# A hybrid encoder step on one core: factors of the scan queued behind splits of weights, the last 32 products with tokens stationary, eight warming products

## The chip, the cores and the metric

The kernel runs on one core of a Trainium2 chip. The metric is the device time of one execution in microseconds (us), as the median of several runs. TensorE (PE) multiplies, VectorE (DVE) and ScalarE (ACT) work element by element, GpSimd (POOL) does small copies and sums, and SyncE (SP) issues most of the DMAs. Each engine runs its own queue in the order that the scheduler gave it, and waits there for semaphores.

## The reference

One layer for 256 prompt tokens and 32 sample tokens, 288 columns in all, with 2048 features:

```python
xn   = rmsnorm(x, norm_mix_pre)
proj = xn @ w_in             # columns: u_pool 1024 | z 2048 | xBC 2560 | dt 32
y_pool = pool_mixer(u, ...)  # trailing means, one matmul per group
y_ssd  = ssd_mixer(z, xbc, dt_raw, ...)   # conv, chunked scan, gate silu(z), norm
x    = x + rmsnorm(concat[y_pool, y_ssd] @ w_out, norm_mix_post)
up   = causal_dwconv(rmsnorm(x, norm_ffn_pre) @ w_up)
x    = x + rmsnorm((silu(gate) * val) @ w_down, norm_ffn_post)
# inside the scan, per head, l and s positions of a chunk:
lmat  = exp(acum[l] - acum[s]) masked causally
y     = (C B^T * lmat) (x * dt) + C h_prev exp(acum) + D x
```

The outputs are y for both groups of tokens and the new states. Everything is in float32.

## The kernel before

Activations lie with features on the partitions and the 288 tokens along the free axis. A product in full precision is made of three: weights and activations are each split into a high part (`whi`, `xn`'s first half) and the rest (`wlo`), and `mm3` (L144 to L146) multiplies high by high, high by low and low by high. `split_w` makes the parts of a tile of weights in pieces of 1024 columns: ACT copies to the high part (L137), DVE subtracts for the rest (L138).

`project` computes 256 output features from all 2048 inputs: two fetched tiles of weights, four splits, 24 products of 288 columns per split, into two PSUM tiles `acc`. Projects 1 to 7 of the loop make the inner x of the scan; their results are evacuated by DVE (L359, L360, into `ebuf`), go through a convolution of four taps (`conv`, L372), a tanh and `xs` (L377, L378). Projects 8 to 15 make the gates z (evacuated at L555). Behind each project `scan(i)` runs, i being the project's number. The scan works on heads in fours, eight of them, with numbers q from 0 to 7:

- `four_in(q)` loads `gb` (log decays), `h0t` (state) and `xw` by SP, and makes the factors: `ce` (ACT Exp, DVE L489), `xw` (DVE L492, times dt), `m` (ACT Relu in twelve pieces and one Exp of 1664 columns at L499, DVE L501 times C B^T). It is called at the projects in SCAN_IN = {5, 6, 7, 8, 9, 11, 12, 13}.
- `four_out` issues 16 products `py` (L523) and adds them to xs on DVE (L528). At the projects in SCAN_OUT = {7, 9, 12, 14} two fours are put out, directly behind the project's last product on PE.

The scheduler orders the instructions of each engine by a simulation of its own; `tc.issue_after(x)` keeps what stands under it behind x in the order, `tc.high_priority(offset=...)` pulls it ahead, `tc.keep_in_program_order` fixes it. `last_in[0]` is the latest evacuation.

At the start, six calls of a product of ones (`idle`, L260, two passes of PE each) run until the first input is there. At the end, the last 256 output features of the down projection are computed apart: for the first six tiles of input all three products go to `low`; for the 16 others, low by high goes to `low` for all tokens, high by both parts of the activations goes to `run_a` for tokens 128 to 287 (L1172), and the same for tokens 0 to 127 to `run_b` (32 products of 256 columns, L1185, weights stationary). DVE adds these to `part` (L1115), ACT squares (L1118), a product with a column of constants (`mean`) sums over the features (`psum_f`, L1086), ACT takes the root (`rf`, L1100), DVE inverts. The tokens are turned to rows by PE (`pft`, L1080), and DVE scales and adds the residual (`y_out`, L1129), but one tile of 512 columns goes over PE: residual by identity (L1208) plus rows by diag(rf) (L1215). The part of the prompt tokens in each output tile b is 128 tokens in a row, b·128 to b·128 + 127.

## Time and profile before

| | before |
|---|---|
| median of 3 runs | 1233.65 us (1233.14 to 1234.08) |
| profiled execution, own time | 1235.27 us |
| its span | 1233.0 us |
| PE busy | 1225.3 us (99%) |
| DVE busy | 888.2 us (72%) |
| ACT busy | 670.2 us (54%) |
| POOL busy | 276.3 us (22%) |

The span is the time between the first and the last instruction of the profiled execution; its own time holds what lies around it too. In a row of the timeline the first number is the start in us from the beginning of the span, the second the duration from the first start to the last end, then the engine, the line, the operation and the tiles (out<-in); "x8" says that eight instructions in a row stand together, and brackets tell how long the engine stood idle before and what released it. A PE row's duration is longer than the distance to the next, since matmuls are pipelined.

### The profile page before, as it was taken

The page shows a single profiled execution, that of the slowest core. Times are in us where ns is not written, and L with a number is a line of the kernel's source. Part 1 is how long each engine was busy: PE and PEld are TensorE (multiplying, and loading weights), DVE is VectorE, ACT ScalarE, POOL GpSimd, SP SyncE. Part 2 cuts the span into 40 slices and gives each one's busy share as a digit, 9 for nine tenths or more (in the row PEclk, how much of TensorE's full clock was granted, in tenths as well). Part 3 has the DMA queues.
Part 4 walks back from the last instruction along what each step waited for, and adds up shares of the span by engine and source line. Part 5 has one row for each costly group of instructions (what it writes and reads, how often), then busy time and mean ns, then how long its engine had stood idle before and what let it go on. Part 6 is the DMA issues. An engine that isn't in the chain of part 4 may idle for free.

```text
span 1233.0 us, 25222 instructions
## 1 busy us (share of the span) xinstructions
PE 1225.3 (99%) x10059; PEld 1213.7 (98%) x10059; DVE 888.2 (72%) x1484; ACT 670.2 (54%) x1011; POOL 276.3 (22%) x427
## 2 busy tenths in 40 slices
PE   9999999999999999999999999999999999999998
PEld 9999999999999999999999999999999999999997
DVE  8899998989664599887776744446777777765555
ACT  8557787546554466645554544334555454554443
POOL 6395442131341200221211200001112121101110
PEclk9999999999999999999999999999999999999999
DMA  9668785466576555676655455555555555576763
GB/s 356 197 208 307 263 279 172 149 243 221 199 242 216 191 177 201 200 228 181 208 185 171 166 185 179 169 191 188 189 172 175 188 184 172 175 252 198 217 190 118
DMA packets 87589, 249.82 MB, mean 203 GB/s; under 512 B 45712, under 2 KB 51920, under 8 KB 65200
## 3 DMA queue, kind: packets, MB, share of 16 engines
q1 hardware_dynamic: 83184, 240.78, 58.3%
q0 software_dynamic: 3712, 6.95, 1.9%
q8 instruction: 78, 1.28, 0.4%
q10 hardware_dynamic: 576, 0.49, 0.1%
q14 instruction: 39, 0.32, 0.1%
HBM read 236.23 MB, written 11.95 MB: 201 GB/s over the span
## 4 chain that ended last, share of the span: by engine, by line
PE 63%; DMA 1%; DVE 1%; ACT 0%; issue 0%; DVEq 0%
PE acc L144 20%; PE acc L145 20%; PE acc L146 20%; DMA st<-xs_d 1%; PE acc_x L145 0%; PE acc_x L144 0%; PE acc_x L146 0%; PE run_a L1172 0%; PE low L1170 0%; PE run_b L1185 0%; DVE rm L247 0%; PE low L146 0%; PE low L145 0%; PE low L144 0%; DVE sh L836 0%; PE y_ps L1215 0%
## 5 line engine op out<-in xcount | busy, mean ns | idle before, releaser
L138 DVE TENSOR_TENSOR wlo<-raw,whi 128x1024 fp32r<-128x1024 f32 (+1 forms) x386 | 461.3, 1198 | 245.6 <-ACT whi L137 245.3
L137 ACT ACTIVATE whi<-raw 128x1024 fp32r<-128x1024 f32 (+1 forms) x386 | 396.9, 1031 | 349.2 <-PE acc L145 283.4
L145 PE MATMUL acc<-hn,whi 128*128 128x288 f32 x1360 | 382.9, 286 | 0.0
L146 PE MATMUL acc<-hn,wlo 128*128 128x288 f32 x1360 | 382.7, 286 | 0.0
L144 PE MATMUL acc<-hn,whi 128*128 128x288 f32 x1360 | 382.2, 286 | 0.3 <-ACT hn L926 0.3
L144 PEld LDWEIGHTS acc<-hn,whi 128*128 128x128 f32 x1360 | 254.2, 189 | 0.8 <-ACT hn L926 0.7
L145 PEld LDWEIGHTS acc<-hn,whi 128*128 128x128 f32 x1360 | 254.7, 189 | 0.1
L146 PEld LDWEIGHTS acc<-hn,wlo 128*128 128x128 f32 x1360 | 254.6, 189 | 0.0
L144 PE MATMUL acc<-xn,whi 128*128 128x288 f32 x686 | 197.2, 289 | 0.0
L145 PE MATMUL acc<-xn,whi 128*128 128x288 f32 x686 | 195.6, 287 | 0.0
L146 PE MATMUL acc<-xn,wlo 128*128 128x288 f32 x686 | 192.3, 287 | 0.6 <-DVE wlo L138 0.6
L144 PE MATMUL acc<-fa,whi 128*128 128x288 f32 x660 | 188.8, 286 | 0.0
L145 PE MATMUL acc<-fa,whi 128*128 128x288 f32 x660 | 188.8, 286 | 0.0
L146 PE MATMUL acc<-fa,wlo 128*128 128x288 f32 x660 | 188.8, 286 | 0.0
L980 POOL COPY fc_stage<-ebuf 128x4 f32<-128x4 f32 x88 | 28.7, 326 | 463.4 <-DVE ebuf L979 401.2
L144 PEld LDWEIGHTS acc<-xn,whi 128*128 128x128 f32 x686 | 130.1, 190 | 1.4 <-issue 0.9
L145 PEld LDWEIGHTS acc<-xn,whi 128*128 128x128 f32 x686 | 130.1, 190 | 0.3
L146 PEld LDWEIGHTS acc<-xn,wlo 128*128 128x128 f32 x686 | 128.3, 190 | 1.0 <-DVE wlo L138 1.0
L144 PEld LDWEIGHTS acc<-fa,whi 128*128 128x128 f32 x660 | 124.7, 189 | 0.0
L145 PEld LDWEIGHTS acc<-fa,whi 128*128 128x128 f32 x660 | 124.7, 189 | 0.0
L146 PEld LDWEIGHTS acc<-fa,wlo 128*128 128x128 f32 x660 | 124.7, 189 | 0.0
L984 ACT ACTIVATE fc<-ebuf,pf 128x290 f32<-128x290 f32 x88 | 54.4, 622 | 78.7 <-DVE ebuf L979 78.7
(312 smaller groups left out, 1799.8 us busy)
## 6 DMA issues: line engine op xcount, KB each, us to landing
raw<-in_w_up SPq DMA_DIRECT2D x80, 1024.0 KB, 4.8
raw<-in_w_in SPq DMA_DIRECT2D x38, 1024.0 KB, 5.1
raw<-in_w_down SPq DMA_DIRECT2D x32, 1024.0 KB, 4.8
raw<-in_w_out SPq DMA_DIRECT2D x23, 1024.0 KB, 5.1
raw<-in_w_down SPq DMA_DIRECT2D x16, 768.0 KB, 4.5
raw<-in_w_up SPq DMA_DIRECT2D x8, 896.0 KB, 4.7
gb<-g_d SPq DMA_DIRECT2D x8, 832.0 KB, 6.6
raw<-in_w_first SPq DMA_DIRECT2D x5, 768.0 KB, 8.5
```

Source lines behind the costliest of these rows:

```text
L137: act.activation(hi, raw[:, k : k + n, :], AF.Copy)
L138: dve.tensor_tensor(lo, raw[:, k : k + n, :], hi.bitcast(F32), op=ALU.subtract)
L144: pe.matmul(out, wh, hi, start=start, stop=False)
L145: pe.matmul(out, wh, lo, start=False, stop=False)
L146: pe.matmul(out, wl, hi, start=False, stop=stop)
L980: pool.tensor_copy(fc_stage[:, :, :, i], e[:, 256:324].rearrange("p (s c) -> p s c", c=34)[:, :, 0:2])
L984: act.activation(c, e[:, 0:290], AF.Identity, bias=pf[:, 3, i : i + 1], scale=pf[:, 0, i : i + 1])
```

## The change

Three parts.

1. `four_in` is split. It keeps the loads; a new `four_mul` makes the factors and takes a split of weights (`splits` collects ACT's copies) behind which they are issued, besides the latest evacuation. The first four of a pair is made at the second SCAN_IN project of the pair, behind the last split issued; the second at the SCAN_OUT project, behind the fourth last. In project 6 both are made, behind the last two splits.
2. In the last 32 products the tokens are stationary and the weights move, so that `run_b` holds tokens on the partitions. Its tokens are the even ones of the prompt, `run_a`'s the odd ones and the sample's. What `low` gave to the even tokens is copied by ACT (`even`) and added by two products with the identity. The square sum of these features comes from ACT's accumulator (`total`), that of the earlier ones from a product (`rb`); the gains of the last 256 features are loaded as a row (`g_row`, by POOL), and DVE multiplies by them (`fg`). The tile that goes over PE is made in two halves, and its output DMA is issued by ACT. Output tiles hold every second token.
3. The warming calls are eight instead of six.

```diff
+    splits = []
...
-                act.activation(hi, raw[:, k : k + n, :], AF.Copy)
+                splits.append(act.activation(hi, raw[:, k : k + n, :], AF.Copy))
...
-    for i in range(6):
+    for i in range(8):
         tc.keep_in_program_order(pe.matmul(idle, ones, ones, start=True, stop=True))
...
-        with tc.issue_after(last_in[0].ins):
+        return gb, xw, h0t, ce, m
+
+    def four_mul(q, gb, xw, h0t, ce, m, after):
+
+        with tc.issue_after(last_in[0].ins), tc.issue_after(after.ins):
             act.activation(ce, gb[:, :, 384:], AF.Exp)
...
-    ready = []
+    loads, ready = [], []
...
+    def four_next(after):
+        q, tiles = loads.pop(0)
+        ready.append((q, four_mul(q, *tiles, after)))
...
         if i in SCAN_OUT:
+            if loads:
+                four_next(splits[-4])
...
-            ready.append((q, four_in(q)))
+            loads.append((q, four_in(q)))
+            if len(loads) == 2:
+                four_next(splits[-2 if i == 6 else -1])
+                if i == 6:
+                    four_next(splits[-1])
...
+    g_row = ebuf[0][:, : 2 * P]
+    pool.dma_start(out=g_row, in_=g_last.broadcast_to([P, 2 * P]))
...
-                sp.dma_start(out=ft[2 * q + b][:, :n], in_=fd[b * P : (b + 1) * P, c])
+                sp.dma_start(out=ft[2 * q + b][:, :n], in_=fd[b:NP_:2, c])
...
     def run_of(a, c):
-        return a.rearrange("p s (r j) -> p s j r", r=2)[:, :, c.start // 2 : c.stop // 2, :]
+        return a[:, :, c].rearrange("p s c -> p c s")
...
+    even = [out_tile("even") for _ in range(2)]
+    for j in range(2):
+        act.activation(even[j][:, :P], part[KD - 2 + j][:, 0:NP_:2], AF.Copy)
...
-    for j in range(2):
-        c = slice(j * P, (j + 1) * P)
-        for i, (k, hi, lo) in enumerate(held):
+    for i, (k, hi, lo) in enumerate(held):
+        for s in range(2):
             tc.keep_in_program_order(
-                pe.matmul(pb[j], hi[:, c], run_of(f2[k], B), start=k == K_RUN, stop=k == HALF - 1)
+                pe.matmul(
+                    pb, f2[k][:, s, B], turns(hi),
+                    start=i + s == 0, stop=i == len(held) - 1 and s == 1,
+                )
             )
+        if i == 1:
+            for j in range(2):
+                tc.keep_in_program_order(
+                    pe.matmul(by_turns(pb)[:, j, :], even[j][:, :P], ident, start=False, stop=False)
+                )
...
+            act.activation(rb, p_f[1][:, 0:1], AF.Identity, bias=eps_t)
...
+    tc.keep_in_program_order(
+        dve.tensor_tensor(last[0][:, : 2 * P].rearrange("p (r j) -> p r j", r=2), by_turns(pb), halves(g_row), op=ALU.mult)
+    )
+    act.activation(sq[:, : 2 * P], pb, AF.Square, accum_out=total)
+    act.activation(rf[:, 0:1], total, AF.Sqrt, bias=rb, scale=1.0 / D_MODEL)
+    dve.reciprocal(rf[:, 0:1], rf[:, 0:1])
+    y_ps = [acc_ps.tile([P, 2 * P], F32, tag="acc", name="y_ps") for _ in range(2)]
...
+    for i, p_ in enumerate(y_ps):
+        pe.matmul(p_, diag, halves(ft[2])[:, i, :], start=False, stop=True)
+        act.activation(halves(xr[2])[:, i, :], p_, AF.Copy)
...
-    sp.dma_start(out=y_rows[:, 1, :], in_=xr[2])
+    act.dma_start(out=y_rows[:, 1, :], in_=xr[2])
```

**Where instructions stand, first place: project 9's end.** On DVE before, a four's factors (ce, xw, m) stand behind the first z of project 8 (acc_2063); these are the factors of the second four that project 9 puts out.

```order
L555 TENSOR_TENSOR z_2182<-acc_2063,rstd_124 128x288 [waits PE_49]
L489 TENSOR_TENSOR ce_2225<-ce_2225,bc_772 128x128
L492 TENSOR_TENSOR xw_2222<-xw_2222,tok_734 128x768 [waits DMAHW6_49,DMAHW4_49]
L501 TENSOR_TENSOR m_2226<-m_2226,cbt_795 128x1664 [waits Activation_49]
```

On DVE after, they stand behind both z of project 9 (acc_2241, acc_2242).

```order
L140 TENSOR_TENSOR wlo_2507<-raw_2504,whi_2506 128x1024 [waits DMAHW6_49,PE_49,Activation_49]
L561 TENSOR_TENSOR z_2359<-acc_2241,rstd_124 128x288 [waits PE_49]
L374 SCALAR_TENSOR_TENSOR conv_2170<-ebuf0_110,pah_122,conv_2170 128x291 [waits DVE_49]
L182 STREAM_TRANSPOSE blocks_1991<-xs_1980 128x288 [waits DMASW2_49,DMASW1_49,DMASW3_49,DMASW0_49,DVE_49]
L374 SCALAR_TENSOR_TENSOR conv_2187<-ebuf1_112,pah_122,conv_2187 128x291 [waits Activation_49,Pool_49]
L561 TENSOR_TENSOR z_2361<-acc_2242,rstd_124 128x288 [waits PE_49]
L495 TENSOR_TENSOR ce_2209<-ce_2209,bc_774 128x128
L498 TENSOR_TENSOR xw_2206<-xw_2206,tok_736 128x768 [waits DMAHW5_49,DMAHW3_49]
L507 TENSOR_TENSOR m_2210<-m_2210,cbt_797 128x1664
L140 TENSOR_TENSOR wlo_2511<-raw_2504,whi_2510 128x1024 [waits Activation_49]
```

On PE before, at the same place, from the project's last product to the second four's first:

```order
L146 MATMUL acc_2258<-xn_609,wlo_2324 128x288
L523 MATMUL py_2379<-m_2043,xw_2039 64x256 [waits DMAHW0_49,PE_49]
...
L523 MATMUL py_2380<-ce_2042,h0t_2037 64x32 x2
L523 MATMUL py_2381<-m_2226,xw_2222 64x256 [waits DMAHW4_49,PE_49]
L523 MATMUL py_2381<-m_2226,xw_2222 64x256
```

and after:

```order
L148 MATMUL acc_2242<-xn_611,wlo_2308 128x288
L529 MATMUL py_2381<-m_2045,xw_2041 64x256 [waits DMAHW0_49,PE_49]
...
L529 MATMUL py_2382<-ce_2044,h0t_2039 64x32 x2
L529 MATMUL py_2383<-m_2210,xw_2206 64x256 [waits DMAHW3_49,DVE_49,PE_49]
L529 MATMUL py_2383<-m_2210,xw_2206 64x256
```

The order on PE is the same, and the second four's first product has a wait for DVE that it had not. The same wait stands at the second four's first product in projects 12 and 14, where DVE has one split and the project's two z right ahead of the factors; in project 7 there is none.

**Second place: DVE at the evacuation of project 6** (ebuf4, ebuf5), before:

```order
L359 TENSOR_TENSOR ebuf4_673<-acc_1652,rstd_124 128x256 [waits PE_49]
L138 TENSOR_TENSOR wlo_1900<-raw_1897,whi_1899 128x1024 [waits DMAHW6_49,Activation_49]
L360 TENSOR_TENSOR ebuf4_673<-acc_1652,rstd_124 128x32
...
L359 TENSOR_TENSOR ebuf5_674<-acc_1653,rstd_124 128x256 [waits PE_49]
L360 TENSOR_TENSOR ebuf5_674<-acc_1653,rstd_124 128x32
L489 TENSOR_TENSOR ce_1817<-ce_1817,bc_772 128x128
L492 TENSOR_TENSOR xw_1814<-xw_1814,tok_734 128x768 [waits DMAHW7_49,DMAHW0_49]
L501 TENSOR_TENSOR m_1818<-m_1818,cbt_795 128x1664 [waits DMAHW3_49]
L138 TENSOR_TENSOR wlo_1904<-raw_1897,whi_1903 128x1024 [waits Activation_49]
```

and after:

```order
L361 TENSOR_TENSOR ebuf5_676<-acc_1637,rstd_124 128x256 [waits PE_49]
L362 TENSOR_TENSOR ebuf5_676<-acc_1637,rstd_124 128x32
L140 TENSOR_TENSOR wlo_1848<-raw_1841,whi_1847 128x1024 [waits Activation_49]
L495 TENSOR_TENSOR ce_1634<-ce_1634,bc_774 128x128
L498 TENSOR_TENSOR xw_1631<-xw_1631,tok_736 128x768 [waits DMAHW1_49,DMAHW0_49]
L507 TENSOR_TENSOR m_1635<-m_1635,cbt_797 128x1664
L495 TENSOR_TENSOR ce_1801<-ce_1801,bc_774 128x128
L498 TENSOR_TENSOR xw_1798<-xw_1798,tok_736 128x768 [waits DMAHW7_49,DMAHW0_49]
L140 TENSOR_TENSOR wlo_1902<-raw_1899,whi_1901 128x1024 [waits DMAHW6_49,Activation_49]
L379 SCALAR_TENSOR_TENSOR xs_1593<-tanh_1600,conv_1595 128x256 [waits Activation_49]
L380 SCALAR_TENSOR_TENSOR xs_1593<-tanh_1600,conv_1595 128x32
L507 TENSOR_TENSOR m_1802<-m_1802,cbt_797 128x1664 [waits DMAHW3_49,Activation_49]
```

Before, two splits of project 7 are done around one four's factors. After, one split comes ahead of both fours' factors, and the next two are between and behind them.

**Third place: PE's last rows**, before:

```order
L1185 MATMUL run_b<-fa,whi 128x256 x13
L1086 MATMUL psum_f<-mean,fsq 128x1
L1208 MATMUL y_ps<-xr,ident 128x512
L1080 MATMUL pft<-ident,part 128x128
L1086 MATMUL psum_f<-mean,fsq 128x1
L1080 MATMUL pft<-ident,part 128x128
L1215 MATMUL y_ps<-ft,diag 128x512
```

and after:

```order
L1221 MATMUL psum_f<-mean,fsum 128x1
L1203 MATMUL run_b<-whi,fa 128x256 x16
L1240 MATMUL y_ps<-xr,ident 128x256 x2
L1243 MATMUL y_ps<-ft,diag 128x256 x2
```

Sums and transposes of run_b's tokens are no longer there, and the two products of y are four of half the width.

More of the change, by code (lines that the diff above doesn't have):

```diff
@@ L60, in body @@
     w_down,
+    g_last,
     y_rows,
@@ L1046, in body @@
             t = apool.tile([P, 512], F32, tag="a", name="xr")
-            sp.dma_start(out=t, in_=x1d[b * P : (b + 1) * P, 512 * q : 512 * (q + 1)])
+            sp.dma_start(out=t, in_=x1d[b:NP_:2, 512 * q : 512 * (q + 1)])
             xr.append(t)
@@ L1057, in body @@
     A, B = slice(P, NT), slice(0, P)
-    AB = (((1, P, P), (2, NP_, NS)), ((0, 0, P),))
+    AB = ((1, slice(1, NP_, 2)), (2, slice(NP_, NT)))
     rf = const.tile([P, 3], F32, name="rf")
+    g_row = ebuf[0][:, : 2 * P]
+    out_tile = lambda name: fp.tile([P, 290], F32, tag="fc", bufs=6, name=name)
+    pool.dma_start(out=g_row, in_=g_last.broadcast_to([P, 2 * P]))
     p_f = [aux([P, 4], "psum_f")]
@@ L1069, in to_tokens, with turn @@
             for b in range(2):
-                sp.dma_start(out=ft[2 * q + b][:, :n], in_=fd[b * P : (b + 1) * P, c])
+                sp.dma_start(out=ft[2 * q + b][:, :n], in_=fd[b:NP_:2, c])
             sp.dma_start(out=ft_s[NS * q : NS * (q + 1), :n], in_=fd[NP_:NT, c])
-    def turn(j, run):
-        for b, o, n in AB[run]:
+    def turn(j):
+        for b, tok_ in AB:
             c = slice(j * P, (j + 1) * P)
-            t = part[KD - 2 + j][:, o : o + n]
+            t = part[KD - 2 + j][:, tok_]
             if b == 2:
@@ L1080, in turn, with feature_sums @@
                 ins = pe.transpose(last[b][:, c], t, ident)
-            if run == 0:
-                tc.keep_in_program_order(ins)
-    def feature_sums(sq, run, first_, last_):
-        if run:
-            pe.matmul(p_f[1][:, 0:1], sq[:, B], mean[:, 0:1], start=first_, stop=last_)
-            return
+            tc.keep_in_program_order(ins)
+    def feature_sums(sq, first_, last_):
         keep = (lambda ins: ins) if first_ else tc.keep_in_program_order
-        keep(pe.matmul(p_f[0][:, 1:2], sq[:, P:NP_], mean[:, 0:1], start=first_, stop=False, skip_group_check=True))
+        keep(pe.matmul(p_f[0][:, 1:2], sq[:, 1:NP_:2], mean[:, 0:1], start=first_, stop=False, skip_group_check=True))
         for q in range(4):
@@ L1096, in feature_sums, with final_rstd @@
             )
-    def final_rstd(run):
-        c = slice(0, 1) if run else slice(1, 3)
-        act.activation(rf[:, c], p_f[run][:, c], AF.Sqrt, bias=eps_t)
+    def final_rstd():
+        c = slice(1, 3)
+        act.activation(rf[:, c], p_f[0][:, c], AF.Sqrt, bias=eps_t)
         dve.reciprocal(rf[:, c], rf[:, c])
@@ L1108, in run_of, with run_out @@
     def run_of(a, c):
-        return a.rearrange("p s (r j) -> p s j r", r=2)[:, :, c.start // 2 : c.stop // 2, :]
-    def run_out(j, run, p_, sq):
+        return a[:, :, c].rearrange("p s c -> p c s")
+    def run_out(j, p_, sq):
         t = KD - 2 + j
-        c = B if run else A
-        for i in range(2):
-            ins = dve.tensor_tensor(part[t][:, c], part[t][:, c], p_[:, i, :], op=ALU.add)
-            if run and j:
-                tc.keep_in_program_order(ins)
-        act.activation(sq[:, c], part[t][:, c], AF.Square)
-        act.activation(part[t][:, c], part[t][:, c], AF.Copy, scale=g_ffn_post[:, t : t + 1])
+        p_ = p_.rearrange("p (c s) -> p s c", s=2)
+        for o, c in ((part[t][:, 1::2], slice(NS // 2, None)), (part[t][:, NP_::2], slice(0, NS // 2))):
+            for i in range(2):
+                dve.tensor_tensor(o, o, p_[:, i, c], op=ALU.add)
+        act.activation(sq, part[t], AF.Square)
+        act.activation(part[t], part[t], AF.Copy, scale=g_ffn_post[:, t : t + 1])
     def y_out(q, b):
@@ L1125, in y_out @@
         for o, n, src in (
-            ((0, 512, f_),) if q < 3 else ((0, 2 * P, f_[:, : 2 * P]), (2 * P, 2 * P, last[b]))
+            ((0, 512, f_),) if q < 3 else ((0, 2 * P, f_[:, : 2 * P]), (2 * P, 2 * P, last[b][:, : 2 * P]))
         ):
@@ L1151, in body @@
     p1 = [acc_ps.tile([P, NT], F32, tag="acc", name="low") for _ in range(2)]
-    pa = [acc_ps.tile([P, 2, NT - P], F32, tag="acc", name="run_a") for _ in range(2)]
-    pb = [acc_ps.tile([P, 2, P], F32, tag="acc", name="run_b"), aux([P, 2, P], "run_b")]
+    pa = [acc_ps.tile([P, 2 * (NT - P)], F32, tag="acc", name="run_a") for _ in range(2)]
+    pb = acc_ps.tile([P, 2 * P], F32, tag="acc", name="run_b")
     fsq = [fp.tile([P, NT], F32, tag="fr", bufs=2, name="fsq") for _ in range(2)]
@@ L1159, in body @@
             tokens_before(KD - 2)
-            feature_sums(fsum, 0, True, False)
+            feature_sums(fsum, True, False)
         for piece in split_w(raw, kb, n, 256):
@@ L1177, in body @@
         dve.tensor_tensor(part[t], part[t], p1[j], op=ALU.add)
+    even = [out_tile("even") for _ in range(2)]
     for j in range(2):
-        run_out(j, 0, pa[j], fsq[j])
+        act.activation(even[j][:, :P], part[KD - 2 + j][:, 0:NP_:2], AF.Copy)
+    for j in range(2):
+        run_out(j, pa[j], fsq[j])
     last.update({1: acc_ps.tile([P, 2 * P], F32, tag="acc", name="pft"), 2: aux([P, 2 * P], "pft")})
-    for j in range(2):
-        c = slice(j * P, (j + 1) * P)
-        for i, (k, hi, lo) in enumerate(held):
+    p_f.append(aux([P, 4], "psum_f"))
+    rb = const.tile([P, 1], F32, name="rb")
+    for i, (k, hi, lo) in enumerate(held):
+        for s in range(2):
             tc.keep_in_program_order(
-                pe.matmul(pb[j], hi[:, c], run_of(f2[k], B), start=k == K_RUN, stop=k == HALF - 1)
-            )
-            if j == 0 and i == 13:
-                for i in range(2):
-                    feature_sums(fsq[i], 0, False, i == 1)
-                final_rstd(0)
-            if j == 1 and i == 2:
-                for i in range(2):
-                    turn(i, 0)
-                act.activation(ft_s[P - NS :, 2 * P :], last[2][P - NS :, :], AF.Copy)
-        if j:
-            for q in range(4):
-                y_out(q, 1)
-        run_out(j, 1, pb[j], fsq[j])
+                pe.matmul(
+                    pb, f2[k][:, s, B], turns(hi),
+                    start=i + s == 0, stop=i == len(held) - 1 and s == 1,
+                )
+            )
+        if i == 1:
[3 more added lines that the diff above has]
+                )
+        if i == 4:
+            for j in range(2):
+                feature_sums(fsq[j], False, j == 1)
+            final_rstd()
+        if i == 7:
+            for j in range(2):
+                turn(j)
+            act.activation(ft_s[P - NS :, 2 * P :], last[2][P - NS :, :], AF.Copy)
+            tc.keep_in_program_order(pe.matmul(p_f[1][:, 0:1], fsum[:, 0:NP_:2], mean[:, 0:1], start=True, stop=True))
+            act.activation(rb, p_f[1][:, 0:1], AF.Identity, bias=eps_t)
+    for q in range(4):
+        y_out(q, 1)
     tc.keep_in_program_order(
@@ L1202, in body @@
     sp.dma_start(out=y_rows[:, 8, :], in_=xr_s)
-    p_f.append(acc_ps.tile([P, 4], F32, tag="acc", name="psum_f"))
-    last[0] = acc_ps.tile([P, 2 * P], F32, tag="acc", name="pft")
-    feature_sums(fsum, 1, True, False)
-    y_ps = acc_ps.tile([P, 512], F32, tag="acc", name="y_ps")
-    feature_sums(fsq[0], 1, False, False)
-    tc.keep_in_program_order(pe.matmul(y_ps, ident, xr[2], start=True, stop=False))
-    feature_sums(fsq[1], 1, False, True)
-    final_rstd(1)
-    for j in range(2):
-        turn(j, 1)
-    diag = fp.tile([P, NT], F32, tag="fr", bufs=2, name="diag")[:, :P]
+    last[0], sq, diag = (out_tile(n) for n in ("fg", "sq_t", "diag"))
+    diag = diag[:, :P]
+    total = const.tile([P, 1], F32, name="total")
+    tc.keep_in_program_order(
[6 more added lines that the diff above has]
+    for i, p_ in enumerate(y_ps):
+        tc.keep_in_program_order(pe.matmul(p_, ident, halves(xr[2])[:, i, :], start=True, stop=False))
     act.activation(diag, ident, AF.Copy, scale=rf[:, 0:1])
-    pe.matmul(y_ps, diag, ft[2], start=False, stop=True)
-    act.activation(xr[2], y_ps, AF.Copy)
+    for i, p_ in enumerate(y_ps):
+        pe.matmul(p_, diag, halves(ft[2])[:, i, :], start=False, stop=True)
+        act.activation(halves(xr[2])[:, i, :], p_, AF.Copy)
     for q in (0, 2, 3):
         y_out(q, 0)
-    sp.dma_start(out=y_rows[:, 1, :], in_=xr[2])
+    act.dma_start(out=y_rows[:, 1, :], in_=xr[2])
     ffn.close()
@@ L1264, in _layout @@
         w_down=weights(np.asarray(i["w_down"])[0]),
+        g_last=np.asarray(i["norm_ffn_post"]).reshape(1, -1)[:, D_MODEL - 2 * P :],
     )
@@ L1291, in heads @@
         return _np.ascontiguousarray(a.T).reshape(1, 1, HEADS, 64, P)
-    y_p = _np.ascontiguousarray(y[:, :8].reshape(P, 2, D_MODEL).transpose(1, 0, 2)).reshape(1, NP_, D_MODEL)
+    y_p = _np.ascontiguousarray(y[:, :8]).reshape(1, NP_, D_MODEL)
     y_s = _np.ascontiguousarray(y[:, 8].reshape(4, NS, 512).transpose(1, 0, 2)).reshape(1, NS, D_MODEL)
```

## The prediction

> **What bounds the kernel now.** I read the page first: span and busy shares.

> ```profile
> span 1233.0 us, 25222 instructions
> PE 1225.3 (99%) x10059; PEld 1213.7 (98%) x10059; DVE 888.2 (72%) x1484; ACT 670.2 (54%) x1011; POOL 276.3 (22%) x427
> ```

> TensorE (PE) is busy for 99% of the span, so time can only come from three sources: PE waiting, PE running more passes or running slowly, and the two ends of the run, where PE is not the last. The profiled execution took 1235.27 us, 2.27 around its span, and stands 1.62 above the median of 1233.65; I sum against 1235.27 and subtract 1.62 at the end.

> Then the stretch with the scan, by windows (length, then busy time of PE, weight loads, DVE, ACT, POOL, then the clock):

> ```profile
> 100.00:240.00 140.00, 139.42 (x1261) 135.71 (x1261) 127.06 (x213) 105.92 (x211) 49.90 (x75) 1.00 0.70 244
> ```

> Here DVE is busy for 127.06 of 140, not the page's 72%. What DVE does late here can stop PE. PE's timeline shows it stopped twice for a split of weights:

> ```profile
> 152.50 0.29 PE L145 MATMUL acc<-xn,whi 128*128 128x288 f32 x1
> 152.98 0.39 PE L146 MATMUL acc<-xn,wlo 128*128 128x288 f32 x1 [0.20 <-DVE wlo L138]
> ...
> 213.95 0.29 PE L144 MATMUL acc<-xn,whi 128*128 128x288 f32 x1
> 214.62 0.39 PE L146 MATMUL acc<-xn,wlo 128*128 128x288 f32 x1 [0.38 <-DVE wlo L138]
> ```

> Two products normally start 0.12 apart (24 in 2.94, from the rows at 125.00 and 127.94 below). Here it is 0.48 and 0.67: 0.36 + 0.55 = 0.91 lost. Both are behind factors of the scan, and this is all that moving the factors can win.

> **The change, part by part.**

> *Second four of a pair, projects 9, 12 and 14.* Before, its factors (ce, xw, m) stand on DVE behind the evacuation of an earlier project. Now they stand behind this project's own last z, while PE's first py product of that four follows PE's last product by only one four. Durations on DVE and PE:

> ```profile
> 106.99 0.29 PE L146 MATMUL acc<-xn,wlo 128*128 128x288 f32 x1
> ...
> 107.32 0.42 DVE L359 TENSOR_TENSOR ebuf<-acc,rstd 128x256 f32<-128x256 f32 x1
> ...
> 107.76 0.28 DVE L489 TENSOR_TENSOR ce<-ce,bc 128x128 f32<-128x128 f32 x1
> ...
> 148.47 0.45 DVE L555 TENSOR_TENSOR z<-acc,rstd 128x288 f32<-128x288 f32 x1
> ...
> 149.04 0.95 DVE L492 TENSOR_TENSOR xw<-xw,tok 128x768 f32<-128x768 f32 x1
> 149.91 1.88 DVE L501 TENSOR_TENSOR m<-m,cbt 128x1664 f32<-128x1664 f32 x1
> 151.71 1.22 DVE L138 TENSOR_TENSOR wlo<-raw,whi 128x1024 fp32r<-128x1024 f32 x1
> ...
> 158.35 0.29 PE L146 MATMUL acc<-xn,wlo 128*128 128x288 f32 x1
> 158.57 1.73 PE L523 MATMUL py<-m,xw 128*64 128x256 f32 x24
> 160.36 0.63 PE L523 MATMUL py<-m,xw 128*64 128x256 f32 x4
> 160.71 0.45 DVE L555 TENSOR_TENSOR z<-acc,rstd 128x288 f32<-128x288 f32 x1
> ```

> Let t be the start of a project's last product. The evacuation starts at t + 0.33 (106.99 to 107.32). From z's start to m's end come z and ce, 0.57 (148.47 to 149.04), xw 0.87, m by its row 1.88, and 0.05 until PE starts, which is 151.71 + 1.22 = 152.93 against 152.98: t + 3.70. PE gets there without waiting at t + 0.22 + 1.79 = t + 2.01 (158.35, 158.57, 160.36). The wait is 1.69, three times: **+5.07**. While PE waits nothing is behind it but the next project's products, which all move with it; the split that they need next, 1.22 on DVE behind m, is covered by that four's py and 24 products. ACT's part (Relu, Exp) is queued a project earlier and hides in ACT's 34 idle us of the window above; without that cover m would wait for an Exp.

> At project 9 DVE is late besides: its z began at 160.71 where t + 0.33 is 158.68, 2.03 late, behind a split, a z, a transpose and a conv. The same rows stand ahead of z in the new order (one conv more): **+2.03**. At 12 and 14 I take z as on time, since in the new order only a split and the pair of z stand right ahead of the factors, and since the lateness of before there came from m waiting for ACT's Exp, by the rows grouped over 100 to 240:

> ```profile
> L501 DVE TENSOR_TENSOR m<-m,cbt 128x1664 f32<-128x1664 f32 x8 | 15.1, 1888 | 7.9 <-ACT m L499 7.9
> ```

> Those 7.9 us of DVE's time come free. The ends are 0 and 2.03 at each.

> *Project 7, both fours behind two splits.* The new order puts the evacuation of project 6 ahead of the split that project 7 needs for its third quarter, then ce, xw, m and ce, xw ahead of the next.

> ```profile
> 125.00 0.29 PE L146 MATMUL acc<-xn,wlo 128*128 128x288 f32 x1
> ...
> 127.94 0.29 PE L146 MATMUL acc<-xn,wlo 128*128 128x288 f32 x1
> ```

> These are the first products that need those splits' wlo tiles. Project 6's last product started 51 products before 125.00, 118.76; its evacuation starts at 119.09 and takes 0.44 (107.32 to 107.76); then come a split 1.22, ce 0.28, xw 0.87, m 1.80, ce 0.28, xw 0.87, split and release 1.27, which ends at 126.12 by the rows' lengths and at 125.88 with 0.08 off for each of three overlaps (as 149.91 + 1.88 against 151.71): PE waits 0.88. The next: xs 0.44 (as an evacuation), m 1.80, split 1.22 end at 129.3 against 127.94 + 0.88, 0.45 more. **+1.33**, low end 0.88.

> *Waits that go.* Both stops above, **−0.91**.

> The scan together: 5.07 + 2.03 + 1.33 − 0.91 = **+7.5**.

> *Head: four more warming passes* (two calls of two passes).

> ```profile
> 0.85 2.90 PE L260 MATMUL idle<-const-float32-1.0 128*128 128x128 f32 x12 [0.85 <-PEq L1273]
> ...
> 3.33 0.42 PE L260 MATMUL idle<-const-float32-1.0 128*128 128x128 f32 x1
> ...
> 4.25 2.29 PE L291 MATMUL acc<-xs,raw 128*128 128x288 f32 x4 [0.49 <-DVE xs L289]
> ...
> 8.25 0.85 PE L146 MATMUL acc<-xn,wlo 128*128 128x288 f32 x3
> ...
> 8.94 0.29 PE L146 MATMUL acc_x<-xn,wlo 128*128 128x288 f32 x1
> ```

> Twelve passes start from 0.85 to 3.33, 0.2255 apart. Four more put the last at 4.23 and the first product at 4.46, not 4.25: +0.2. But products run 0.24 apart up to 8.25 (three in 0.85 less the last's tail) and at 0.12 from 8.94 on, 4.69 after the end of the 0.49 gap. Warming passes that close the gap let such a count begin at 0.85: full rate from 5.54, and 3.4 us at double rate are worth 1.7. Supply limits it:

> ```profile
> 8.43 0.96 DVE L301 TENSOR_TENSOR wlo<-raw,whi 128x768 fp32r<-128x768 f32 x1 [0.21 <-ACT whi L300]
> ...
> 7.00:8.00 1.00, 1.00 (x6) 1.00 (x5) 0.80 (x3) 1.00 (x3) 0.00 (x0) 1.00 1.02 394
> ```

> In the window 7 to 8 ACT is full, and DVE waits for it at 8.43; a PE that comes 1.5 earlier would outrun its splits. I take **−1.1**, near the upper row since only the last of the slow products are short of splits; ends +0.2 and −1.5. The window's clock column says 1.00 while only six products ran in a microsecond, so the slow rate doesn't show in it. [...]

> *Tail.* The last 32 products keep their number and their 256 columns, with the roles of weights and tokens exchanged. PE adds two products of 128 columns, four passes, for the copies, and drops behind run_b the transposes and sums of the 128 tokens.

> ```profile
> 1218.55 1.26 DVE L1115 TENSOR_TENSOR part<-part,run_a 128x160 f32<-128x160 f32 x4
> ...
> 1218.90 1.73 PE L1185 MATMUL run_b<-fa,whi 128*128 128x256 f32 x14
> ...
> 1225.04 1.10 PE L1208 MATMUL y_ps<-xr,ident 128*128 128x512 f32 x2
> 1225.16 0.60 DVE L1115 TENSOR_TENSOR part<-part,run_b 128x128 f32<-128x128 f32 x2
> 1225.67 0.75 DVE L1200 SCALAR_TENSOR_TENSOR xr_s<-ft_s,rf,xr_s 128x512 f32<-128x512 f32 x1
> 1225.79 0.31 ACT L1118 ACTIVATE fsq<-part 128x128 f32<-128x128 f32 x1 [1.54 <-DVE part L1115]
> 1226.57 0.26 ACT L1100 ACTIVATE rf<-psum_f,eps_t 128x1 f32<-128x1 f32 x1
> 1226.87 0.16 DVE L1101 RECIPROCAL rf<-rf 128x1 f32<-128x1 f32 x1 [0.45 <-ACT rf L1100]
> 1227.06 0.40 ACT L1214 ACTIVATE diag<-ident,rf 128x128 f32<-128x128 f32 x1 [0.23 <-DVE rf L1101]
> 1227.52 1.13 PE L1215 MATMUL y_ps<-ft,diag 128*128 128x512 f32 x2 [0.60 <-ACT diag L1214]
> 1228.68 0.60 ACT L1216 ACTIVATE xr<-y_ps 128x512 f32<-128x512 f32 x1 [1.22 <-PE y_ps L1215]
> ...
> 1229.73 0.41 SPq L1132 DMA_DIRECT2D out<-xr  x1
> ```

> 512 columns twice take 1.10, so 128 take 0.14 and four 0.55; I count 0.3 of that, since one transpose of 128 (0.14) and some of its wait among run_b's products get cheaper when nothing of another run is queued there; an estimate, between 0 and 0.55. So run_b's last product, 0.1 before DVE's 1225.16, ends 0.3 later, at 1225.36. The copies have their source at 1218.55 at the latest, and PE wants them four products (0.5) behind 1218.90: two on ACT, at 0.31 each as for 128 columns, are just covered; without that PE would wait. Before, 1.41 passed from DVE's first use of run_b to the root (1225.16 to 1226.57); now a Square of 256 columns with its sum stands there, 0.45 on ACT (between 0.31 for 128 and 0.60 for 512), so the root starts near 1225.9 and the reciprocal would be free at 1226.2. On DVE xr_s (0.75) and the product with the gains (0.4, as z) stand ahead of it, which makes it 1226.5 where it was 1226.87. From there the same four steps of y follow as before, and the last issue comes near 1228.8, not 1229.73: **−0.9**, with ends −0.4 (DVE's pair fully ahead, copies at 0.60) and −1.3 (neither).

> *Costed at nothing.* POOL's load of the gains: POOL is 78% idle by the page, and its queue holds only copies to an output behind it; were it late, fg would wait, in the tail alone. The loads of gb, xw and h0t on SP stand where they stood but for one fetch of weights that changes place with them; four buffers of weights cover that, and without them PE would wait for a raw tile. Interleaved token rows change addresses, not sizes.

> Sum: 7.5 − 1.1 − 0.9 = +5.5: 1240.8 against 1235.27, and **1239.1** against the median.

> **The rivals.**

> *Factors in time (faster).* If DVE has m done when PE arrives, the stops at 9, 12, 14 and 7 do not exist and what is left is −0.91 − 1.1 − 0.9 = −2.9: 1230.7. For it: 7.9 us of DVE's waits go, and DVE has 13 idle us in 140. Against: m's chain begins with an evacuation that can't start before PE's last product, and even a free DVE needs 3.70 where PE needs 2.01. It decides where the chain loses 1.69, that is if z no longer stands ahead in time or py is not PE's next work. Chance 0.12.

> *DVE as late at 12 and 14 as at 9.* +4.06: 1243.2. For it: the 127 of 140 and the same kind of work; against: the 7.9 that go. Chance 0.10.

> *The clock falls back after the stops.* Each stop is 1.7 to 3.7 long. The trace has only the head for it: 4.69 at half rate costs 2.35 once; after project 9's stop that gives 1241.4. Against it: the 0.49 gap is the longest stop the trace shows, so nothing tells. Chance 0.05. [...]

> *The warming passes do nothing.* Then the head is +0.2, not −1.1: 1240.4, inside the main case.

> **How the numbers follow.** A difference below 0.2%, 2.5 us, is about what a measurement can't tell from no change. Main case 0.70, with 1235.9 (5.07 + 0.88 − 0.91 − 1.5 − 1.3 = +2.2) to 1241.2 (+2.03 at one of 12 and 14). It ends within 0.2% in 0.01 of that; the 0.03 that are left are sums that cancel, within 0.2% too. The range from 1235.6 to 1243.4 holds main case, late DVE and clock: 0.83 with their tails cut; only the faster rival lies outside. Faster 0.12, same 0.04, slower 0.84.

> **What would show it.** In the changed profile: PE waits for DVE's m at the second four's first py in projects 9, 12 and 14 alone, 3.7, 1.7 and 1.7; two short waits for wlo in project 7; none left at 152 and 214; the product after the warming passes at about 4.5 and full rate before 7; a root within a microsecond of run_b's end. The prediction is wrong if the py rows show no wait for m, or if these waits add up to under 3 or over 10 us.

## The result, and the profile after

The changed kernel takes 1243.56 us (median; 1241.56 to 1245.13) against 1233.39 for the kernel before: 0.79% slower, with a 95% interval of 0.66% to 0.92%. The prediction was 1239.1, with a range of 1235.6 to 1243.4: the right sign and most of the right places, about half the size. The median lies 0.16 us past the range's upper end as an absolute time; 0.79% above the 1233.65 that the prediction started from is that end, 1243.4. One of the six executions of the scan's part alone (below) took 2155.81 us at a granted clock of 0.56, and one of the kernel before in the same group 1271.03 at 0.95; both are left out of every figure here. The profiled execution took 1244.38, its span is 1242.7.

The head of the page and its table of stretches, to be read against the first rows of the prediction (for 100 to 240 us the columns are length, PE, weight loads, DVE, ACT, POOL, clock, DMA share, GB/s):

```profile
span 1242.7 us, 25236 instructions
PE 1227.0 (99%) x10065; PEld 1215.7 (98%) x10065; DVE 886.8 (71%) x1485; ACT 671.7 (54%) x1013; POOL 279.2 (22%) x428
...
100.00:240.00 140.00, 131.37 (x1180) 127.36 (x1179) 119.12 (x201) 102.28 (x205) 46.27 (x72) 0.99 0.67 233
```

Over the whole span nothing is to be seen: 99% PE. In the scan's stretch PE fell from 139.42 to 131.37 of 140, and the clock from 1.00 to 0.99. What PE waited for, by its waits (total, number, longest):

```profile
PE py L529 <- issue: 5.3, 2, 3.8
PE py L529 <- DVE m L507: 2.7, 1, 2.7
PE y_ps L1243 <- ACT diag L1241: 1.1, 1, 1.1
PE idle L262 <- PEq L1302: 0.8, 1, 0.8
PE acc L148 <- DVE wlo L140: 0.8, 3, 0.5
```

Three waits of py are new, in projects 9, 12 and 14; project 7 has two short ones for wlo. Two of the three are put down to "issue", which means only that the view found no event; the order of DVE tells what they were. PE and DVE at project 9:

```profile
158.38 0.29 PE L148 MATMUL acc<-xn,wlo 128*128 128x288 f32 x1
158.60 1.73 PE L529 MATMUL py<-m,xw 128*64 128x256 f32 x24
160.15 0.40 PE L529 MATMUL py<-ce,h0t 128*64 128x32 f32 x8
164.31 0.65 PE L529 MATMUL py<-m,xw 128*64 128x256 f32 x4 [3.75 <-issue]
```

```profile
158.16 1.22 DVE L140 TENSOR_TENSOR wlo<-raw,whi 128x1024 fp32r<-128x1024 f32 x1
159.30 0.45 DVE L561 TENSOR_TENSOR z<-acc,rstd 128x288 f32<-128x288 f32 x1
159.66 0.52 DVE L374 SCALAR_TENSOR_TENSOR conv<-ebuf,pah,conv 128x291 f32<-128x291 f32 x1
160.09 0.47 DVE L182 STREAM_TRANSPOSE blocks<-xs 128x288 f32<-128x288 f32 x1
160.49 0.48 DVE L374 SCALAR_TENSOR_TENSOR conv<-ebuf,pah,conv 128x291 f32<-128x291 f32 x1
160.88 0.45 DVE L561 TENSOR_TENSOR z<-acc,rstd 128x288 f32<-128x288 f32 x1
...
162.32 1.89 DVE L507 TENSOR_TENSOR m<-m,cbt 128x1664 f32<-128x1664 f32 x1
```

m ends at 164.21, py starts at 164.31. The last z started 2.17 after it could (158.38 + 0.33 = 158.71), behind the five rows above it; the rest is the chain z, ce, xw, m. At project 12 PE stood still for less, but what came behind it was slow. PE's first rows behind that wait, and the same stretch by windows:

```profile
206.33 0.79 PE L529 MATMUL py<-m,xw 128*64 128x256 f32 x4 [2.68 <-DVE m L507]
206.90 1.07 PE L529 MATMUL py_a<-m,xw 128*64 128x256 f32 x4
...
206.30:209.60 3.30, 3.27 (x33) 2.61 (x33) 2.84 (x6) 3.05 (x7) 0.00 (x0) 0.56 0.51 119
235.00:237.50 2.50, 0.98 (x26) 0.87 (x22) 2.50 (x3) 0.79 (x3) 0.00 (x0) 1.00 0.44 184
```

The first of these windows has a granted clock of 0.56: half rate. The second four's py take 3.23 us there, against 1.89 at project 9 and 1.87 before. At project 14 the wait is short (1.58) and the clock stays at 1.00.

Where the 9.7 us of span went, by how far the same instruction on PE had moved at each place (before to after):

| place | us | forecast |
|---|---|---|
| head, up to the product with mean (37.73 to 37.06) | −0.67 | −1.1 |
| project 7, two waits for wlo | +1.16 | +1.33 |
| project 9, wait before the second four | +3.95 | +3.72 |
| project 12, wait 2.85, half rate 1.36 in py and 0.28 behind | +4.49 | +1.69 |
| project 14, wait | +1.77 | +1.69 |
| waits for wlo at 152 and 214 that went | −1.12 | −0.91 |
| output projection, two waits for wlo at 346 and 349 | +0.70 | 0 |
| a wait for ACT's msq at 439 that went | −0.77 | 0 |
| tail, from run_b to the span's end | +0.2 | −0.9 |

### The profile page after: what moved, and what is told of

Read it like the earlier page. It is cut to its first block, busy times and chain, and to the rows that moved or that the text cites. A ratio compares the mean times of both kernels' runs of the same rounds, so it can differ in the third digit from the quotient of the medians.

```text
span 1242.7 us, 25236 instructions
## 1 busy us (share of the span) xinstructions
PE 1227.0 (99%) x10065; PEld 1215.7 (98%) x10065; DVE 886.8 (71%) x1485; ACT 671.7 (54%) x1013; POOL 279.2 (22%) x428
## 3 DMA queue, kind: packets, MB, share of 16 engines
q8 instruction: 78, 1.28, 0.4%
## 4 chain that ended last, share of the span: by engine, by line
PE 63%; DVE 1%; DMA 1%; ACT 0%; issue 0%; DVEq 0%
PE acc L146 20%; PE acc L148 20%; PE acc L147 20%; DMA st<-xs_d 1%; PE acc_x L148 0%; PE acc_x L146 0%; PE acc_x L147 0%; PE low L1184 0%; PE run_a L1186 0%; PE run_b L1203 0%; DVE rm L249 0%; DVE xr L1143 0%; PE low L148 0%; PE low L147 0%; PE low L146 0%; DVE sh L852 0%
## 5 line engine op out<-in xcount | busy, mean ns | idle before, releaser
L146 PE MATMUL acc<-hn,whi 128*128 128x288 f32 x1360 | 382.2, 286 | 0.3 <-ACT hn L942 0.3
L146 PEld LDWEIGHTS acc<-hn,whi 128*128 128x128 f32 x1360 | 254.2, 189 | 0.7 <-ACT hn L942 0.7
L146 PE MATMUL acc<-xn,whi 128*128 128x288 f32 x686 | 197.1, 289 | 0.0
L146 PE MATMUL acc<-fa,whi 128*128 128x288 f32 x660 | 188.8, 286 | 0.0
L146 PEld LDWEIGHTS acc<-xn,whi 128*128 128x128 f32 x686 | 129.7, 189 | 1.5 <-issue 0.9
L146 PEld LDWEIGHTS acc<-fa,whi 128*128 128x128 f32 x660 | 124.7, 189 | 0.0
```

What stands on the lines that cost most here:

```text
L146: pe.matmul(out, wh, hi, start=start, stop=False)
```

## The experiments

**The parts alone.** Scan, warming calls and tail, each put into the kernel before by itself. The scan's part:

```diff
+            if loads:
+                four_next(splits[-4])
...
+            if len(loads) == 2:
+                four_next(splits[-2 if i == 6 else -1])
```

> The kernel before with the scan's part of the change alone (six warming calls, the old tail). Theory A, the scan carries the loss: from the two traces the scan's stretch lost 1.16 us in project 7, 3.94 at project 9, 4.49 at project 12 (2.66 of waiting and 1.8 of products at half rate), 1.77 at project 14, and won 1.12 from two waits for wlo that went; about 10 us in all, so some 1243.5 and 0.7 to 0.9% slower. Rival B, the parts add to each other (the earlier start of the head shifts PE against DVE and makes the waits): then this run is under 7 us slower.

Measured: 1242.38 (the median of five executions), ratio 1.0069 (1.0052 to 1.0087). The scan's part carries the loss without the others, so the parts do not make each other's waits, and theory A holds with one correction. Here project 12 waited 1.75 and lost nothing to the clock; half rate was at project 9. Windows of this run:

```profile
163.20:165.00 1.80, 1.80 (x10) 1.15 (x12) 1.80 (x3) 0.29 (x1) 0.17 (x1) 0.50 0.26 41
165.00:168.00 3.00, 3.00 (x31) 2.94 (x28) 3.00 (x11) 0.93 (x3) 0.69 (x3) 0.50 0.89 303
...
206.40:208.00 1.60, 1.60 (x26) 1.31 (x28) 1.60 (x3) 1.60 (x6) 0.00 (x0) 1.00 0.68 225
```

The warming calls:

```diff
-    for i in range(6):
+    for i in range(8):
```

> The kernel before with eight warming calls instead of six and nothing else. Theory A: PE is at the product with mean (prs, 37.73 us before) 0.67 us earlier, full rate is there before 6 us instead of 8.9, and of some 1.5 us won there 0.8 go in two waits for wlo near 14 and 23 us; time -0.7, within the noise. Rival: the calls win nothing and only start the first product later, +0.2.

Measured: 1234.46 against 1233.36, ratio 1.0007 (0.9996 to 1.0019): no gain. The product with mean came at 36.01, 1.7 earlier than in the profile of before, but so it did with six calls in the two other runs of this group that have six: 35.97 in the scan's part alone, 36.16 in the tail's.

The tail:

```diff
+    act.activation(sq[:, : 2 * P], pb, AF.Square, accum_out=total)
...
+    act.dma_start(out=y_rows[:, 1, :], in_=xr[2])
```

> The kernel before with the new tail alone. Theory A, read from the two traces: from run_b's first product to the last issue 0.2 us less than before, and 0.3 more until the span's end, so no difference that can be measured (-0.3 to +0.5). Rival, by the prediction: -0.9.

Measured: ratio 0.9999 (0.9989 to 1.0010). No difference, as theory A has it; the interval is too wide to exclude the −0.9 by the time alone, so the trace decides. From run_b's first product to the end of the last output issue, 11.24 us before (1218.90 to 1230.14), 11.02 here (1217.90 to 1228.92): −0.2. From there to the span's end it is 3.26 where it was 2.84, because the last output landed 2.29 us after the end of its issue and not 1.87. Over the whole tail nothing is won: 14.28 against 14.08.

**Where the second four's factors stand.** One condition changed in the changed kernel; `evac_before[0]` is the evacuation of the project before:

```diff
-        with tc.issue_after(last_in[0].ins), tc.issue_after(after.ins):
+        with tc.issue_after(evac.ins), tc.issue_after(after.ins):
...
-                four_next(splits[-4])
+                four_next(splits[-4], evac_before[0])
```

> The changed kernel, with one thing different: the second four's factors are issued behind the evacuation of the project before and not behind this project's own z. Theory A, that place is the cause: no wait of the second four's py for m, no half rate at project 12, and a time of 1233 to 1235, 9 us under the changed kernel's. Rival C, factors behind splits crowd DVE wherever they stand: the waits for m turn into waits for wlo of the next projects, and the time stays over 1237.

Measured: 1235.87, ratio 1.0015 (1.0005 to 1.0025), 7.7 us under the changed kernel and 0.9 above theory A's range. No py waits for m and the clock stays full: the place behind the project's own z is the cause of all three waits. But rival C has a share: in project 9 both fours' factors now stand one behind the other on DVE, and PE waits for splits. By its waits:

```profile
PE acc L148 <- DVE wlo L140: 2.8, 4, 1.1
PE y_ps L1246 <- ACT diag L1244: 1.1, 1, 1.1
```

Two of the four are those of project 7, which the changed kernel has too (0.52 and 0.17 here). The other two are new, 1.02 in project 9 and 1.10 in project 12. The first of these, by PE's timeline:

```profile
155.16 0.29 PE L147 MATMUL acc<-xn,whi 128*128 128x288 f32 x1
156.47 0.39 PE L148 MATMUL acc<-xn,wlo 128*128 128x288 f32 x1 [1.02 <-DVE wlo L140]
```

**Is the half rate PE's own doing?** Products of ones fill the waits; nothing else is changed in the code:

```diff
+        for _n in range(fill):
+            tc.keep_in_program_order(pe.matmul(ys[0][:, 0:P], ones, ones, start=True, stop=True))
         for y, w_, v_, go, end in ops:
...
+                         fill={9: 17, 12: 12, 14: 7}.get(i, 0) if n else 0)
```

> The changed kernel with products of ones (into the PSUM tile that the second four overwrites next) in front of the second four's py: 17 calls in project 9, 12 in project 12, 7 in project 14, each about 0.22 us, so that PE is busy for most of each wait and still gets there before m. Theory A, the slow py and products behind a wait come from PE having stood still: the three waits keep their lengths (3.9, 1.5 to 2.7 and 1.7 us from the first four's last py to the second four's first), no product behind them is at half rate, and the time falls by 1 to 2.5 us against the changed kernel, to 1241 to 1242.5. Rival, the slow products come from DVE, ACT or DMAs using the same memories at that time: they stay slow, and the time stays at 1243.5.

Measured: 1242.86 and ratio 1.0077 (1.0064 to 1.0089). PE's timeline at project 9, and windows at the places where the other runs were slow:

```profile
159.98 4.06 PE L526 MATMUL py<-const-float32-1.0 128*128 128x128 f32 x34
163.97 0.65 PE L531 MATMUL py<-m,xw 128*64 128x256 f32 x4
...
164.00:166.00 2.00, 2.00 (x34) 1.67 (x34) 2.00 (x4) 0.45 (x1) 0.18 (x1) 1.00 0.34 72
...
206.00:208.00 2.00, 2.00 (x35) 1.58 (x33) 2.00 (x6) 1.97 (x6) 1.35 (x1) 1.00 0.49 114
```

The clock is 1.00 at both, and the second fours of projects 9, 12 and 14 all take 1.89: the slow products come from PE having stood still, and the rival, contention on DVE's, ACT's and DMA's side, falls, since those were about as busy there. All timed executions agree: the mean granted clock is 0.999 to 1.000 in all five of this kernel, and at most 0.998 in twelve of the thirteen executions of the two kernels with bare waits, the changed one and the scan's part alone (0.999 in the other).

The time, however, fell by only 0.4 against the changed kernel in the same group, inside the noise and less than expected. One reason stands in the trace: the products of ones ran on past m. At project 12:

```profile
202.93 1.89 DVE L507 TENSOR_TENSOR m<-m,cbt 128x1664 f32<-128x1664 f32 x1
...
203.22 2.94 PE L526 MATMUL py<-const-float32-1.0 128*128 128x128 f32 x24
...
206.10 0.65 PE L531 MATMUL py<-m,xw 128*64 128x256 f32 x4
```

m ended at 204.82, and py started 1.28 later, where 0.10 was enough at project 9 of the changed kernel. The second fours' waits, from the first four's last py, were 4.14, 3.03 and 1.91 here; 0.17, 1.18 and about 0.1 of them are the filling's own, some 1.4 us in all. By this estimate the sum in the table below would be near 7.6 without it. So this run shows where the half rate comes from, and not what it costs in time. The scheduler also gave DVE another order around project 12: no split waits for ACT there, and z starts at 201.13, on time. The wait without the filling's overrun would be about 1.8 there, near the 1.69 forecast.

**The changed kernel once more.**

> The changed kernel once more, with another profile. Theory A, the clock decides by windows of time that don't start with the kernel: the waits at 9 and 14 have the same lengths within 0.1 us, the stretch at half rate may lie behind another one of the three waits, and the time is 1243.5 with a spread of 3 us. Rival, project 12 has something of its own: half rate there again and only there.

Measured: 1243.29, ratio 1.0082 (1.0068 to 1.0096). The waits at 9 and 14 are the same (3.97 and 1.80 from the first four's last py). The half rate was at project 9, and project 12's wait was 1.75, not 2.90:

```profile
163.55 0.65 PE L529 MATMUL py<-m,xw 128*64 128x256 f32 x4 [3.75 <-issue]
164.00 0.89 PE L529 MATMUL py_a<-m,xw 128*64 128x256 f32 x4
...
206.00 0.65 PE L529 MATMUL py<-m,xw 128*64 128x256 f32 x4 [1.53 <-DVE m L507]
...
163.60:166.50 2.90, 2.90 (x33) 2.58 (x33) 2.90 (x6) 0.45 (x1) 0.19 (x1) 0.61 0.44 101
```

So project 12 has nothing of its own. The four traces together, in us from the first py to the next project's first product (3.65 before at each place):

| run | project 9 | project 12 | project 14 | sum over before |
|---|---|---|---|---|
| changed kernel | 7.60 | 7.86, half rate | 5.42 | +9.93 |
| changed kernel again | 8.63, half rate | 5.38 | 5.42 | +8.48 |
| scan's part alone | 9.25, half rate | 5.38 | 5.42 | +9.10 |
| waits filled | 7.77 | 6.65 | 5.53 | +9.00, some 1.4 of it the filling's |

Of what the clock takes at 9, much comes back at 12, in the two traces with half rate at project 9: PE reaches project 12 later against DVE, and waits 1.75 instead of 2.90.

**Warming calls, none and twelve**, in the kernel before:

> The kernel before without warming calls. [...] Rival, DVE's and ACT's splits set the pace of the head anyway: the product with mean stays at 36 to 37.7 us and the time within 0.5 us.

> The kernel before with twelve warming calls, 24 passes. Theory A: PE is busy from 0.85 until the calls end, at about 4.6 to 6.5 depending on the clock; full rate by 6.5 at the latest, the first product up to 1 us later than with six, and the time the same within 1 us. Rival, more calls keep the clock at full rate from the first product and the time falls by more than 1 us.

Measured: ratios 1.0007 (0.9998 to 1.0017) and 1.0007 (0.9997 to 1.0016). Nothing that can be told from six. Without calls full rate came at 9.26, later than in any profile with calls (8.90 at the latest), and the product with mean at 37.89, 0.2 past the rival's 37.7; whether the time stayed within the rival's 0.5 us is neither shown nor excluded (the interval ends at 0.17%, 2.1 us). With twelve the first product started at 5.96, 1.7 to 2.0 later than with six and not up to 1; full rate was there before it, at 5.81, and the time didn't fall by the more than 1 us of the rival. All profiles' heads, where "full rate from" is the first step of the clock that the trace records:

| calls | full rate from, us | product with mean at, us |
|---|---|---|
| 0 | 9.26 | 37.89 |
| 6, four profiles | 8.90, 4.31, 5.45, 4.25 | 37.73, 35.97, 36.16, 36.73 |
| 8, six profiles | 5.33, 5.38, 4.87, 6.50, 3.82, 4.86 | 37.06, 36.01, 36.22, 36.55, 36.05, 36.53 |
| 12 | 5.81 | 37.07 |

The profile of before is the one with six calls whose clock came late; it looks like the one without any. Whether two more calls prevent that, as no profile with eight came late, ten profiles can't settle; the times say that it is worth less than 0.2% either way.

**The Square ahead of the gains**, in the tail alone:

```diff
+    act.activation(sq[:, : 2 * P], pb, AF.Square, accum_out=total)
     tc.keep_in_program_order(
         dve.tensor_tensor(last[0][:, : 2 * P].rearrange("p (r j) -> p r j", r=2), by_turns(pb), halves(g_row), op=ALU.mult)
     )
-    act.activation(sq[:, : 2 * P], pb, AF.Square, accum_out=total)
```

> The new tail alone (six warming calls, the scan as before), with ACT's Square of run_b ahead of DVE's product with the gains instead of behind it. Theory A, DVE's product held up the Square by its own 0.42 us: the root comes 0.4 us earlier after run_b's last product, and the last output issue 0.3 to 0.4 earlier. Rival: DVE's product, now later, holds up the reciprocal instead, and the end stays.

Measured in a single execution (1235.64, too few to compare times): from run_b's first product to the root 7.45 us (7.93 with the new tail as it is, 7.67 before), and to the end of the last issue 10.54 (11.02, and 11.24 before). The root gains 0.48 and keeps it up to the last issue. The span doesn't end earlier here, since the last output of this execution landed 3.87 us after its issue. In the next kernel, with the same order, it landed after 2.28, and from run_b's first product to the span's end it is 13.79 (14.25 in the changed kernel, 14.08 before). ACT in the changed kernel, then in this run:

```profile
1235.82 0.38 ACT L1235 ACTIVATE sq_t<-run_b 128x256 f32<-128x256 f32 x1 [2.02 <-DVE fg L1233]
1236.10 0.19 ACT L1235 ACTIVATION_READ_ACCUMULATOR sq_t<-run_b 128x1 f32 x1
```

```profile
1225.48 0.38 ACT L1217 ACTIVATE sq_t<-run_b 128x256 f32<-128x256 f32 x1 [1.56 <-PE run_b L1188]
...
1225.98 0.42 DVE L1219 TENSOR_TENSOR fg<-run_b,ebuf 128x256 f32<-128x256 f32 x1 [0.66 <-ACT sq_t L1217]
```

The two engines read the same PSUM tile one after the other, whichever was written first in the code.

**The likeliest good version**: the first four's factors at their own project, the second's behind the SCAN_OUT project's first split and the evacuation of the project before (as in the experiment on where those factors stand), the Square first. What is new in it:

```diff
-            if len(loads) == 2:
-                four_next(splits[-2 if i == 6 else -1])
-                if i == 6:
-                    four_next(splits[-1])
+            if not ready:
+                four_next(splits[-1])
```

> The changed kernel, where the first four of each pair has its factors at its own SCAN_IN project (as before the change), the second has them behind the first split of the SCAN_OUT project and the evacuation of the project before, and the Square of run_b comes ahead of the product with the gains. Theory A: no wait for m, no wait for wlo over 0.3 us in the scan, so 0.9 us less than the kernel before there, and 0.4 less at the end: 1232 to 1233, at the edge of what can be told from the kernel before. Rival C, factors behind a split only trade one wait for another: waits for wlo of 1 us or more, 1235 to 1236.

Measured: 1232.95 against 1233.06, ratio 1.0000 (0.9990 to 1.0009). In its trace no wait for m or wlo is left between 28 and 330 us, and the stops of before at 152 and 214 are gone, as theory A said. Two waits for wlo stand at 334 and 338 instead, as the changed kernel had in one of its two traces (346 and 349), and they cost 0.9. It makes good the change's loss; that it beats the kernel before is not shown (the interval reaches from −1.2 to +1.1 us). The 0.9 to be won in the scan is also less sure than the profile of before made it: of the five other profiles with the old scan, one has a stop of over 0.1 us for a split in project 9 (near 152), four have one near 214 (one of them another at 193), and one has none.

## Why the prediction was right in sign and too small

- **The wait at projects 9 and 14** was right: 3.72 forecast, 3.95 measured; 1.69 and 1.77. The chain z, ce, xw, m read from before's rows held, and so did DVE's lateness of 2.03 (2.17).
- **Project 12** failed at the step "at 12 and 14 I take z as on time". Its wait was 2.85 or 1.70, over before's, by when PE arrived. In the profile the pair of z started at 202.60 where 201.48 + 0.33 = 201.81 was possible for the second, behind a split that had waited for ACT. That wait stood in the trace of before too, where z came 2.15 late (199.97 where 197.49 + 0.33 was possible); the second pair of rows is from there:

```profile
201.32 1.36 DVE L140 TENSOR_TENSOR wlo<-raw,whi 128x1024 fp32r<-128x1024 f32 x1 [0.38 <-ACT whi L139]
202.60 0.81 DVE L561 TENSOR_TENSOR z<-acc,rstd 128x288 f32<-128x288 f32 x2
```

```profile
198.68 1.37 DVE L138 TENSOR_TENSOR wlo<-raw,whi 128x1024 fp32r<-128x1024 f32 x1 [0.38 <-ACT whi L137]
199.97 0.81 DVE L555 TENSOR_TENSOR z<-acc,rstd 128x288 f32<-128x288 f32 x2
```

  In the changed kernel that is 0.79, and 0.37 more for the first z of the pair: the whole 1.16 above the forecast. So z's lateness at 12 came from a split waiting for ACT, and not only, as the prediction has it, from m waiting for an Exp; in the kernel with filled waits, where this split waits for nothing, z is on time. The rival of late DVE, priced at 4.06 for both projects, was half right: one of two, and 1.16 of 2.03.
- **The clock's fall to half**, a rival with a chance of 0.05 priced at 2.35, happened in all three profiles that have the bare waits. Its direct cost was 1.6 in the first profile; at project 9 it was 1.0 and 1.7 in py, of which up to 1.15 came back at project 12. The argument against it, that the longest stop of before was 0.49, was no argument: it said only that the trace was silent.
- **Project 7 and the two waits that went** were right within about 0.2 each (1.33 forecast, 1.16 measured; −0.91 and −1.12).
- **The head** failed at the step "products run 0.24 apart up to 8.25 ... Warming passes that close the gap let such a count begin at 0.85". The gap starts no count: in the scan's part alone the same gap of 0.49 was followed by full rate from 4.31. What I took for a property of the kernel was this one execution's clock. It was probably also counted twice: as far as the slow head is what put this execution 1.62 above the median, the −1.1 is part of those 1.62, which I took off at the end besides. The column of the clock said 1.00 there because the trace holds no record ahead of the first step, which came at 8.90.
- **The tail** failed in three terms. The four passes cost PE 0.60 more up to y (6.14 to 6.74), where I took 0.3. And the Square did not run beside DVE's product but behind it, 0.46 later; with the accumulator's read of 0.19 the root came 0.96 after DVE's start, where I had 0.54. The last experiment but one gives 0.48 of that back. Third, the sum ended at the last issue, and the last output then landed 2.28 after it instead of 1.87. Whether the interleaved rows did that, which the prediction put at nothing, or two issues 0.2 apart on two engines, no run separates.
- The forecast's sum missed 4.5 of the median. By the parts alone, scan 8.5 (6.4 to 10.7), head and tail near 0 make some 8.5 to 9.5 of the 10.2, against 7.5, −1.1 and −0.9. The rest is inside these intervals. The wait at 346 is there in one execution of the changed kernel and not in the other, and the one at 439 (over 0.1 us) is in three of twelve profiles; no run shows either to belong to the change.

## What to carry to other kernels

When work is moved behind an event, ask whether that event lies less than the work's whole chain ahead of the one who needs it: here m came 3.70 us after the project's last product at the earliest, and PE wanted it 2.01 after; a DVE with nothing else to do could not have mended that. Let the factors go behind an early split, but behind an evacuation that is one project old. Before a slow stretch of one profiled execution is counted as something to win, see whether that execution itself stands above the median: the same microseconds may be in both.

## What the hardware showed that was not expected

Two engines' reads of one PSUM tile went one after the other, at a price of 0.46 us in a tail of 11; it was a wait in the queue, not a slower read (0.38 for the Square in both orders). The Square started at 1235.82 behind DVE's product of 1235.36 in the changed kernel, and DVE's product at 1225.98 behind the Square of 1225.48 with the order turned.
